# Four edits in a two-layer encoder trunk: kept keys and values, unscaled first products, two heads' states on a diagonal, a stacked rank-16 gate

## The chip, the cores and the metric

The kernel is one launch on one core of a Trainium2 chip. The metric is device microseconds per execution, lower is better. A profiled execution gives a trace of the engines: TensorE's multiplications (PE) and its weight loads (PEld), VectorE (DVE), ScalarE (ACT), GpSimd (POOL) and the queue of SyncE that issues the transfers (SP).

## The reference, cut to what matters

Two layers on x of 1024 positions by 1024 channels, all in float32. Each layer normalises x, multiplies it by one wide matrix and splits the columns among three branches: a gated MLP (u, v, z), an attention with low-rank queries, keys and values (8 heads, causal by chunks of 64), and a gated linear attention (GLA, 4 heads with keys of 64 and values of 128). The branches are gated, added and projected.

```python
h = _rmsnorm(x, norm_g[l])              # x * rsqrt(mean(x*x)) * gain, by position
(u_a, v_a, z_a, c_q, c_kv, k_r, z_b, q_c, k_c, v_c, g_c, z_c, gate_logits) = _split_cols(h @ w_in[l])
# attention: q of a position sees all k, v of its chunk and of earlier ones
# GLA, per head: log_a = log_sigmoid(g_c @ w_gate + b) / 16     (g_c has 16 columns)
#   o = (causal part inside the chunk) + q_t @ state
#   state = decay * state + k_s^T @ v
```

## The kernel before, in words

Positions lie in two halves `h` of 512 columns. A product in float32 is made of three products in the one-pass format fp32r: each operand is split into a high part (ScalarE copy) and a low part (subtraction on VectorE), and high x high, low x high and high x low are added in PSUM (`pair` at L497, `split` at L479). A product on plain float32 operands shows as two PE records.

`build` (L1523) lists segments for each layer; `weave` (L514) strews side work between the main products. `Recorder` (L55) only notes the operations. `Order` (L123) then writes one fixed order for every engine's queue: it gives each operation a due time worked back from the products that need it, and a cost, a latency and the free buffers of a shared pool `g` of 94 tiles (L1624). The trace therefore shows all instructions at L1612, and tiles by the names `g`, `mm`, `sc`, `tr`, `av` (the last four are PSUM).

The places that the change and the prediction touch:

- `side_h` (L698) normalises one half: loads of 8 tiles of x, squares on ScalarE and their sums on VectorE, a column sum on TensorE (`stat`), the power -1/2 on GpSimd, a broadcast by a product (`bcast`), then for each tile a multiplication by gain and scale and a split (`mult`). In layer 0 all of half 0 stands ahead of the first product.
- `natural` (L632) is the product with positions as rows: 8 tiles of x, 4 blocks of positions, 3 products each. It makes `main_n1` (L755, 432 columns: low-rank queries, keys and the rank-16 gate input) and `main_va` (L1211, 512 columns), for half 0, then `main_n1` and `main_va` for half 1.
- `side_c` (L795) transposes the 16 gate columns (`gT`), and `side_gates` (L822) multiplies them by the 16 x 256 gate matrix (`wgu`, loaded in `params`, L422), in plain float32 with 16 rows of contraction: 2 products of 512 columns in each of 4 calls.
- `side_core` (L1030) is GLA for a pair of heads `p` and a half: 8 calls over both layers. `state` (L1069) runs the state over the 4 blocks of 128 positions, the two heads in rows 0 to 63 and 64 to 127 of one tile. `o(e)` (L1088), for each head, makes 4 blocks of 128 columns, each from the product inside the chunk (`at` x `vc`, 128 rows of contraction) and that of q with the state (64 rows).
- `side_att` (L1309) is the attention of one half. For each head of half 1, `loads` (L1315) reads the queries, and the keys of both halves; `head_T` (L1342) transposes, scales and splits them; `vsplit` (L1386) splits the values of both halves. The keys and values of half 0 have been through the same steps when half 0 was done.

```python
self.mm(ps[:, c], st["at"][e][:, b], st["vc"][b][:, e * 128:(e + 1) * 128], True, False)
self.mm(ps[:, c], qa[hd, b].rearrange("p c s -> p (c s)"), st["S"][b][hd], False, True)
```

Of the kernel before, what the change touches and what calls it, by code (L numbers as in the profile page):

```python
# [10 lines left out]
F32 = mybir.dt.float32  # L11
# [9 lines left out]
S = 1024  # L21
# [287 lines left out]
class Builder:  # L309
# [29 lines left out]
    def setup(self):  # L339
        nc, cp, I = self.nc, self.cp, self.I  # L340
        self.ident = cp.tile([128, 128], F32, name="ident")
        make_identity(nc, self.ident)
        self.ones = cp.tile([128, 128], F32, name="ones")
        nc.vector.memset(self.ones, 1.0)
        self.mhalf = cp.tile([128, 8], F32, name="mhalf")
        nc.vector.memset(self.mhalf, -0.5)
        self.half = []
        for e in range(2):
            t = cp.tile([128, 128], F32R, name=f"half{e}")
            nc.vector.memset(t.bitcast(F32), 0.0)  # L350
            nc.vector.memset(t[:, 64 * e:64 * e + 64].bitcast(F32), 1.0)
            self.half.append(t)
        self.zero = cp.tile([128, 128], F32, name="zero")
        nc.vector.memset(self.zero, 0.0)

# [66 lines left out]
    def params(self, l):  # L422
        nc, I = self.nc, self.I
        P = self.P[l]

        def ld(name, src, shape):
            t = self.par.tile(list(shape), F32, tag="p_" + name, name=f"{name}{l}", bufs=2)
            self.load(t, src)
            P[name] = t
            return t  # L430

        ld("bg", I["bg"][l], (128, 24))
        ld("cqg", I["cqg"][l], (128, 2))
        ld("ckvg", I["ckvg"][l], (128, 1))
        ld("wgu", I["wgu"][l], (16, 256))
        ld("lng", I["lng"][l], (128, 4))
        ld("bgu", I["bgu"][l], (128, 2))
        ld("og", I["og"][l], (128, 1))
        nb = self.par.tile([128, 2], F32, tag="p_nbgu", name=f"nbgu{l}", bufs=2)
        nc.vector.tensor_scalar(out=nb, in0=P["bgu"], scalar1=-1.0, scalar2=None, op0=ALU.mult)  # L440
        P["nbgu"] = nb
        for n in ("bg", "og"):
            nc.vector.tensor_scalar(out=P[n], in0=P[n], scalar1=0.5, scalar2=None, op0=ALU.mult)
        for x in ("q", "k"):
            gr = ld(x + "gr", I[x + "gr"][l:l + 1].broadcast_to((128, 32)), (128, 32))
# [186 lines left out]
    def natural(self, u, key, width, evac, order=(0, 1)):  # L632
# [3 lines left out]
        def part(h, k):  # L636
            def f():
# [4 lines left out]
                wh, wl = w[k]  # L642
                hh, hl = u["h"][h][k]
                for t in range(NB):
# [7 lines left out]
                if k == 7:  # L652
                    evac(h, box["p"])
            return f

# [41 lines left out]

    def side_h(self, u, h):  # L698
        nc, l = self.nc, u["l"]
# [20 lines left out]
        def stat():  # L720
            ps = self.ps("tr")
            for t in range(NB):
                self.mm(ps[:, t:t + 1], st["s"][:, t * 128:(t + 1) * 128], self.ones[:, 0:1])
            v = self.s((128, NB), "hv")
            nc.vector.tensor_scalar(out=v, in0=ps[:, 0:NB], scalar1=1.0 / D, scalar2=EPS, op0=ALU.mult, op1=ALU.add)
            r = self.s((128, NB), "hr")
            self.rsqrt(r, v)
            dg = st["d"] = self.g()
# [23 lines left out]

        return [loads, sq(range(0, 4)), sq(range(4, 8)), stat, bcast] + [mult(k) for k in range(8)]

    def main_n1(self, u):  # L755
        def evac(h, pss):
# [3 lines left out]
            for t in range(NB):  # L760
                nat = self.g((128, 432))
                self.evac(nat, pss[t])
                s["nat"].append(nat)
# [31 lines left out]
    def side_c(self, u, h):  # L795
        nc, l = self.nc, u["l"]
        s = u["s"][h]
        def gT():
            ps = self.ps("tr")
            for t in range(NB):  # L800
                self.tr(ps[0:16, t * 128:(t + 1) * 128], s["nat"][t][:, 416:432])
            s["gT"] = self.g((16, H))
            nc.vector.tensor_copy(out=s["gT"], in_=ps[0:16])

# [101 lines left out]
    def side_ukv(self, u, h, t):  # L906
# [40 lines left out]
        return fn  # L947

    def evac(self, out, ps):
        self.nc.scalar.copy(out=out, in_=ps)  # L950
# [79 lines left out]
    def side_core(self, u, p, h):  # L1030
# [38 lines left out]
        def state():  # L1069
            dd = u["kt", p, h][3]  # L1070
            U = self.ps("tr")
            for b in range(nu):
                for e in range(2):
                    hd = slice(e * 64, e * 64 + 64)
                    self.mm(U[hd, b * 128:(b + 1) * 128], st["ksn"][:, b * 128 + e * 64:b * 128 + e * 64 + 64],
                            st["vc"][b][:, e * 128:(e + 1) * 128])
            sts = [self.carry[l, p] if h else self.zero]
            big = self.g((128, NB, 128))
            for b in range(nu):
                nx = big[:, b]  # L1080
                if b == NB - 1:
                    nx = self.carry[l, p] = self.s((128, 128), "S", bufs=2)
                nc.vector.scalar_tensor_tensor(out=nx, in0=sts[-1], scalar=dd[:, b:b + 1],
                                               in1=U[:, b * 128:(b + 1) * 128], op0=ALU.mult, op1=ALU.add)
                sts.append(nx)
            st["S"] = sts

        def o(e):  # L1088
            def f():
                qa = u["qt", p, h][0]  # L1090
                hd = slice(e * 64, e * 64 + 64)
                ps = self.ps("sc")
                for b in range(NB):
                    c = slice(b * 128, b * 128 + 128)
                    self.mm(ps[:, c], st["at"][e][:, b], st["vc"][b][:, e * 128:(e + 1) * 128],
                            True, False)
                    self.mm(ps[:, c], qa[hd, b].rearrange("p c s -> p (c s)"), st["S"][b][hd], False, True)
                jk = self.g()
# [8 lines left out]
                                        in1=r.unsqueeze(2).broadcast_to((128, NB, 128)), op=ALU.mult)  # L1107
                st["on"][e] = on
            return f

        def fin(e):
            def f():
                ps = self.ps("tr")
                for b in range(NB):
                    self.tr(ps[:, b * 128:(b + 1) * 128], st["on"][e][:, b])
                y = u.pop(("zc", h, 2 * p + e))
# [94 lines left out]
    def main_va(self, u):  # L1211
        def evac(h, pss):
            for t in range(NB):
                v = self.g()
                self.evac(v, pss[t])
                d = u["vad", h, t] = self.spill("va")
# [92 lines left out]
    def side_att(self, u, h):  # L1309
# [5 lines left out]
        def loads(hd):  # L1315
            x = X[hd] = {}
            cs = slice(hd * 96, (hd + 1) * 96)
            x["n"] = []
            for src in [self.qd[l, h]] + [self.kd[l, f] for f in range(nf)]:
                t4 = self.g((128, NB, 96))  # L1320
                self.load(t4, src[:, :, cs].rearrange("t p d -> p t d"))
                x["n"].append(t4)
            if hd % 2 == 0:
                z = X["z", hd // 2] = self.g()
                self.load(z, u["zbd", h, hd // 2])
                x["v"] = []
                for f in range(nf):
                    vn = self.g((128, NB, 128))
                    self.load(vn, self.vd[l, f][:, :, hd * 64:hd * 64 + 128].rearrange("t p d -> p t d"))
                    x["v"].append(vn)  # L1330
            else:
                x["v"] = X[hd - 1]["v"]

        def masks(hd):
            x = X[hd]
            x["hi"] = []
            for i in range(nf + 1):
                hi = self.g((KM, H), F32R)
                self.load(hi[RM:KM].bitcast(F32), self.cmask[1 + i if i else h])
                x["hi"].append(hi)  # L1340

        def head_T(hd, i):  # L1342
            x = X[hd]
            nat = x["n"][i]
            gain = self.P[l]["gvk" if i else "gvq"]
            ps = self.ps("tr")
            for t in range(NB):
# [4 lines left out]
                                           op1=ALU.subtract)  # L1352
            x["T", i] = (hi, lo)

        def mx(hd, b):
# [30 lines left out]
        def vsplit(hd):  # L1386
# [3 lines left out]
            vs, os = slice(64 * e, 64 * e + 64), slice(64 - 64 * e, 128 - 64 * e)  # L1390
            for vn in x["v"]:
                V = self.g((128, NB, 128), F32R)
                self.split(V[:, :, vs], V[:, :, os], vn[:, :, vs])
                x["V"].append(V)

# [56 lines left out]
        def preps(hd):  # L1452
            out = [lambda: masks(hd)] + [lambda i=i: head_T(hd, i) for i in range(nf + 1)]
            out += [lambda b=b: mx(hd, b) for b in range(NB)]
# [22 lines left out]
        side += [lambda a=a: av(*a) for a in steps[-AVLAG:]]  # L1477
        n0 = 1 + 1 + nf + 1 + NB + 3 + 1
        return side[:n0], side[n0:]
# [43 lines left out]
    def build(self):  # L1523
# [22 lines left out]
        for i, u in enumerate(units):  # L1546
# [6 lines left out]
            if i == 0:  # L1553
                sh = self.side_h(u, 0)
# [137 lines left out]
```

## Time and profile before

| | |
|---|---|
| three executions, median (lowest to highest) | 2029.34 us (2029.3 to 2030.12) |
| the profiled execution | 2029.29 us, span of its instructions 2027.6 us |
| PE, DVE, ACT, POOL busy | 99%, 76%, 50%, 27% of the span |
| moved by DMA | 302.13 MB, 149 GB/s in the mean |

In the trace, PE x16 means 16 records in a row. Ends of products are modelled, so a busy PE may still be slower than its pace. The chain of waits follows the work that ended last back from its end; a row of it tells which engine set the pace in that stretch, and for how long.

### The profile page before, as it was taken

To read this page: it belongs to the slowest core of one execution; us is meant where nothing else is said; L and a number is where in the kernel's file an instruction comes from. 1 tells how busy PE (TensorE), PEld (TensorE's weight loads), DVE (VectorE), ACT (ScalarE), POOL (GpSimd) and SP (SyncE) were. 2 spreads that over 40 slices of the span, in tenths; PEclk is the share of its full clock that TensorE was granted. 3 is DMA by queue.
4 is the path that set the end of the run, shared out by engine and by line. 5 is a ranking of instruction groups with operands and counts; after the bars stand their busy time and mean duration, and the time that the engine had idled before them with its cause. 6 is when DMAs were issued, how large, how long until landed. Compare 5 with 4: busy or idle time off the path is not lost.

```text
span 2027.6 us, 29291 instructions
## 1 busy us (share of the span) xinstructions
PE 2000.4 (99%) x9864; PEld 1648.0 (81%) x9864; DVE 1543.7 (76%) x2779; ACT 1011.8 (50%) x1969; POOL 542.2 (27%) x460
## 2 busy tenths in 40 slices
PE   6999999999999999999999999999999999999999
PEld 5887778888888878888889877788888887887887
DVE  7576666867778988997845856578678799889973
ACT  6565344455456644555434653345445565444541
POOL 1110101001123446665012001110011344567630
PEclk9999999999999999999999999999999999999999
DMA  7262234343533755426743613334435338463362
GB/s 242 87 228 79 73 110 161 130 156 133 185 123 105 244 178 185 131 100 199 248 150 105 206 60 103 110 135 163 138 130 194 112 101 288 133 214 117 102 211 89
DMA packets 216326, 302.13 MB, mean 149 GB/s; under 512 B 63176, under 2 KB 91880, under 8 KB 216176
## 3 DMA queue, kind: packets, MB, share of 16 engines
q1 hardware_dynamic: 216176, 300.26, 44.9%
q8 instruction: 78, 1.28, 0.3%
q14 instruction: 72, 0.59, 0.1%
HBM read 207.76 MB, written 92.43 MB: 148 GB/s over the span
## 4 chain that ended last, share of the span: by engine, by line
PE 91%; DVE 6%; POOL 1%; ACT 1%; issue 1%; DMA 0%; SPq 0%; DVEq 0%; POOLq 0%; ACTq 0%
PE mm L1612 68%; PE sc L1612 10%; PE tr L1612 7%; PE av L1612 6%; DVE g L1612 5%; POOL g L1612 1%; DVE mx L1612 1%; ACT g L1612 1%; DMA g<-xT 0%; POOL hr L1612 0%; DVE negm L1612 0%; SPq L1612 0%; DVE hv L1612 0%; DVEq L1612 0%; POOLq L1612 0%
## 5 line engine op out<-in xcount | busy, mean ns | idle before, releaser
L1612 PE MATMUL mm<-g,g 128*128 128x512 f32 (+1 forms) x6480 | 1588.4, 393 | 2.9 <-ACT g L1612 2.2
L1612 PEld LDWEIGHTS mm<-g,g 128*128 128x128 f32 x6480 | 1197.9, 188 | 248.1 <-issue 5.5
L1612 DVE TENSOR_TENSOR g<-g,g 128x512 fp32r<-128x512 f32 (+5 forms) x1053 | 755.8, 750 | 137.4 <-ACT g L1612 122.9
L1612 POOL TENSOR_TENSOR g<-g,g 128x256 f32<-128x256 f32 (+5 forms) x352 | 419.1, 1211 | 364.4 <-ACT g L1612 260.1
L1612 ACT CAST g<-g 128x512 fp32r<-128x512 f32 (+3 forms) x704 | 401.6, 601 | 229.7 <-DVE g L1612 180.0
L1612 ACT ACTIVATE g<-sc 128x512 f32<-128x512 f32 (+5 forms) x432 | 200.8, 510 | 241.3 <-PE sc L1612 231.6
L1612 PE MATMUL sc<-g,g 64*64 64x64 f32 (+8 forms) x1632 | 264.3, 298 | 0.0
L1612 PEld LDWEIGHTS sc<-g,g 64*64 64x64 f32 (+4 forms) x1632 | 202.8, 172 | 37.9 <-issue 4.7
L1612 DVE TENSOR_TENSOR g<-mm,g 128x512 f32<-128x512 f32 (+1 forms) x176 | 117.5, 673 | 124.3 <-PE mm L1612 74.5
L1612 ACT COPY g<-mm 128x512 f32<-128x512 f32 (+1 forms) x168 | 97.0, 580 | 227.3 <-PE mm L1612 218.2
L1612 PE MATMUL av<-g,g 128*128 128x512 f32 (+3 forms) x672 | 183.9, 362 | 0.3 <-POOL g L1612 0.3
L1612 ACT ACTIVATE g<-g 128x512 f32<-128x512 f32 (+3 forms) x225 | 129.2, 589 | 81.3 <-DVE g L1612 64.2
L1612 PEld LDWEIGHTS av<-g,g 128*128 128x128 f32 x672 | 122.4, 189 | 19.0 <-POOL g L1612 2.1
L1612 DVE SCALAR_TENSOR_TENSOR g<-g,g 128x512 f32<-128x512 f32 (+3 forms) x185 | 129.9, 711 | 7.7 <-ACT g L1612 6.5
L1612 DVE TENSOR_REDUCE mx<-tr 128x1 f32<-128x512 f32 (+1 forms) x192 | 105.0, 570 | 14.9 <-PE tr L1612 13.1
L1612 DVE SCALAR_TENSOR_TENSOR g<-g,mm 128x512 f32<-128x512 f32 x112 | 76.1, 681 | 46.9 <-PE mm L1612 31.0
L1612 PE MATMUL tr<-g,g 128*64 128x128 f32 (+5 forms) x416 | 100.8, 342 | 3.5 <-DVE mx L1612 2.1
L1612 POOL TENSOR_TENSOR qr<-qv,mhalf 128x8 f32<-128x8 f32 x16 | 29.0, 1812 | 280.0 <-DVE qv L1612 280.0
L1612 PEld LDWEIGHTS tr<-g,g 115*128 115x128 f32 (+2 forms) x416 | 62.0, 174 | 25.6 <-DVE mx L1612 6.9
L1612 POOL TENSOR_SCALAR_AFFINE_SELECT g<-g 128x512 f32<-128x512 f32 x16 | 12.3, 768 | 248.8 <-ACT g L1612 243.7
L1612 PE MATMUL tr<-ident,g 128*96 128x128 f32 (+2 forms) x480 | 76.4, 272 | 0.4 <-issue 0.4
L1612 PEld LDWEIGHTS tr<-ident,g 128*96 128x96 f32 (+2 forms) x480 | 57.2, 128 | 17.2 <-issue 1.2
(119 smaller groups left out, 886.6 us busy)
## 6 DMA issues: line engine op xcount, KB each, us to landing
g<-wT SPq DMA_DIRECT2D x176, 256.0 KB
sg<-g SPq DMA_DIRECT2D x96, 256.0 KB
g<-sg SPq DMA_DIRECT2D x96, 256.0 KB
g<-wbr SPq DMA_DIRECT2D x64, 256.0 KB
g<-wo SPq DMA_DIRECT2D x64, 256.0 KB
g<-kd SPq DMA_DIRECT2D x48, 192.0 KB
g<-xT SPq DMA_DIRECT2D x32, 256.0 KB
hd<-g SPq DMA_DIRECT2D x32, 256.0 KB
```

The lines of the kernel that those rows point to most:

```text
L1612: ins = real[op.i] = fn(*a, **k)
```

## The change

Four edits. **Kept keys and values:** half 0's attention stores the transposed, split keys and the split values of each head (three transfers), and half 1's loads them instead of making them again. **Unscaled first products:** in layer 0, the products of half 0 in `main_n1` and `main_va` take x times gain, split without the scale by position; the scale is applied by ScalarE where PSUM is read (`evac_n`). The scaled tiles are still made, later. **Diagonal:** the states of two heads lie on the diagonal of a 128 x 256 tile with zeros beside them, so one product with 128 rows and 256 columns serves both heads; where the state is zero it is left out. **Gate:** high, low and high part of the gate input lie at rows 0, 32 and 64 of one 80-row tile, the high, high and low part of the matrix beside them, so one fp32r product with 80 rows replaces the float32 product.

```diff
# params
-        ld("wgu", I["wgu"][l], (16, 256))
+        w = self.g((80, 256))
+        self.nc.gpsimd.memset(w, 0.0)
+        for r in (0, 32, 64):
+            self.load(w[r:r + 16], I["wgu"][l])
...
+        self.nc.scalar.copy(out=P["wgu"], in_=w)
+        self.nc.vector.tensor_tensor(out=P["wgu"][64:80], in0=w[64:80], in1=P["wgu"][64:80].bitcast(F32),
+                                     op=ALU.subtract)
# natural
-                hh, hl = u["h"][h][k]
+                hh, hl = (u.get(("raw", h)) or u["h"][h])[k]
# side_h
+        def rough(k):
+            def f():
+                gain = self.P[l]["ng"][:, k:k + 1]
+                x, hi, lo = st["x"][k], self.g(dt=F32R), self.g(dt=F32R)
+                nc.scalar.activation(out=hi, in_=x, func=AF.Copy, scale=gain)
+                nc.vector.scalar_tensor_tensor(out=lo, in0=x, scalar=gain, in1=hi.bitcast(F32), op0=ALU.mult,
+                                               op1=ALU.subtract)
+                u.setdefault(("raw", h), []).append((hi, lo))
+            return f
...
+        if early:
+            out[1:1] = [rough(k) for k in range(8)]
# side_c
-            s["gT"] = self.g((16, H))
-            nc.vector.tensor_copy(out=s["gT"], in_=ps[0:16])
+            g = s["gT"] = self.g((80, H), F32R)
+            nc.gpsimd.memset(g.bitcast(F32), 0.0)
+            nc.scalar.copy(out=g[0:16], in_=ps[0:16])
+            nc.scalar.copy(out=g[64:80], in_=ps[0:16])
+            nc.vector.tensor_tensor(out=g[32:48], in0=ps[0:16], in1=g[0:16].bitcast(F32), op=ALU.subtract)
# new, called where main_n1 and main_va read PSUM
+    def evac_n(self, u, h, t, out, ps):
+        if ("raw", h) in u:
+            self.nc.scalar.activation(out=out, in_=ps, func=AF.Copy, scale=u["r", h][:, t:t + 1])
+        else:
+            self.evac(out, ps)
# side_core: state
-                nc.vector.scalar_tensor_tensor(out=nx, in0=sts[-1], scalar=dd[:, b:b + 1],
-                                               in1=U[:, b * 128:(b + 1) * 128], op0=ALU.mult, op1=ALU.add)
+            big = [self.g((128, 2, 256)) for _ in range(2)]
+            own = lambda b, e: big[b // 2][e * 64:e * 64 + 64, b % 2, e * 128:(e + 1) * 128]
+            for t in big:
+                nc.gpsimd.memset(t[0:64, :, 128:256], 0.0)
+                nc.gpsimd.memset(t[64:128, :, 0:128], 0.0)
...
+                for e in range(2):
...
+                        nc.vector.scalar_tensor_tensor(out=nx, in0=own(b, e), scalar=dd[hd, b:b + 1], in1=uc,
+                                                       op0=ALU.mult, op1=ALU.add)
# side_core: o, now by pairs of blocks i instead of by head e
+                for b in (2 * i, 2 * i + 1):
+                    c = (b % 2) * 256
+                    past = h or b
+                    if past:
+                        self.mm(ps[:, c:c + 256], qa[:, b].rearrange("p c s -> p (c s)"), st["S"][b], True, False, True)
+                    for e in range(2):
+                        self.mm(ps[:, c + e * 128:c + (e + 1) * 128], st["at"][e][:, b],
+                                st["vc"][b][:, e * 128:(e + 1) * 128], not past, True, True)
# side_att: masks, head_T, vsplit (loads drops half 0's keys and values)
+            if h:
+                lo = self.g((96, H), F32R)
+                kh, kl, _ = u["kept", hd]
+                self.load(x["hi"][1][0:96].bitcast(F32), kh[0:96])
+                self.load(lo.bitcast(F32), kl[0:96])
+                x["T", 1] = (x["hi"][1], lo)
...
+            if i and not h:
+                u["kept", hd] = [self.spill("kept") for _ in range(3)]
+                for d, t in zip(u["kept", hd], (hi[0:96], lo)):
+                    self.store(d[0:96], t.bitcast(F32))
...
+            if h:
+                V0 = self.g((128, NB, 128), F32R)
+                self.load(flat(V0), u.pop(("kept", hd))[2])
+                x["V"].append(V0)
+            else:
+                self.store(u["kept", hd][2], flat(V))
# build, layer 0
-                segs.append(([], [sh[0], lambda: self.par_ng(0), sh1[0]] + sh[1:], 0, 1))
-                sh1 = sh1[1:5] + [lambda: self.params(0)] + sh1[5:] + [self.setup2]
+                segs.append(([], [sh[0], lambda: self.par_ng(0), sh1[0]] + sh[1:9], 0, 1))
+                sh1 = sh[9:] + sh1[1:5] + [lambda: self.params(0)] + sh1[5:] + [self.setup2]
-            segs.append((n1[:8] + va[:8], sh1, 0.0, 0.7))
+            segs.append((n1[:8] + va[:8], sh1, 0.0 if i else 0.15, 0.7))
```

## Rows read from the trace of the kernel before

**Rows 1.** The page, part 1: busy time, share of the span and instructions.

```profile
PE 2000.4 (99%) x9864; PEld 1648.0 (81%) x9864; DVE 1543.7 (76%) x2779; ACT 1011.8 (50%) x1969; POOL 542.2 (27%) x460
```

**Rows 2.** Waits of PE: who for whom, us in total, times, longest.

```profile
PE tr L1612 <- DVE g L1612: 16.4, 5, 12.4
PE mm L1612 <- ACT g L1612: 2.2, 1, 2.2
PE tr L1612 <- DVE mx L1612: 2.1, 4, 0.6
```

**Rows 3.** The chain of waits, 0 to 60 us: start us, us, what.

```profile
1.71 5.32 DMA g<-xT
...
12.45 1.88 PE tr L1612 x8
...
20.63 1.45 PE mm L1612 x3
22.08 0.36 PE av L1612
22.44 2.07 PE mm L1612 x6
...
27.06 0.11 PE tr L1612 x2
...
27.47 0.56 PE tr L1612 x6
...
31.86 0.86 PE tr L1612 x2
...
43.08 2.08 PE mm L1612 x9
45.16 0.68 PE av L1612 x3
```

**Rows 4.** The chain of waits, 200 to 260 us, in the GLA stretch.

```profile
206.06 3.14 PE sc L1612 x16
...
211.46 0.22 PE sc L1612 x2
...
211.92 0.41 PE sc L1612 x2
...
222.33 2.75 PE mm L1612 x12
...
243.39 2.95 PE mm L1612 x12
```

**Rows 5.** The chain of waits, 402 to 409 us: float32 products with 128 rows.

```profile
402.56 0.89 PE sc L1612 x8
```

**Rows 6.** The chain of waits, 120 to 130 us, around two gate products.

```profile
124.34 1.91 PE sc L1612 x4
126.25 2.27 PE mm L1612 x9
...
129.20 2.04 PE mm L1612 x9
```

**Rows 7.** The chain of waits, 751 us: one head's four transposes.

```profile
751.64 0.44 PE tr L1612 x4
```

**Rows 8.** DVE's groups by form, 0 to 65 us: busy us, mean ns.

```profile
L1612 DVE TENSOR_TENSOR g<-g,g 128x512 fp32r<-128x512 f32 x25 | 16.5, 686 | 1.8 <-ACT g L1612 1.8
L1612 DVE SCALAR_TENSOR_TENSOR g<-g,ng,g 128x512 f32<-128x512 f32 x16 | 11.4, 747 | 0.6 <-ACT g L1612 0.6
L1612 DVE TENSOR_TENSOR g<-g,g 128x432 fp32r<-128x432 f32 x8 | 4.7, 603 | 0.0
```

**Rows 9.** Windows: stretch; PE, PEld, DVE, ACT, POOL busy; clock; DMA.

```profile
200.00:325.00 125.00, 125.00 (x776) 97.95 (x775) 76.26 (x139) 46.83 (x83) 15.66 (x16) 1.00 0.28 91
740.00:940.00 200.00, 198.63 (x949) 162.97 (x947) 175.54 (x237) 101.80 (x209) 136.71 (x107) 1.00 0.44 140
```

**Rows 10.** The state tile: one update on DVE (ns min/median/max).

```profile
L1612 DVE SCALAR_TENSOR_TENSOR g<-S,dd,tr x4: 348/348/349, 232.6 to 1309.2; 128x128 f32<-128x128 f32 x4
```

**Rows 11.** The chain of waits, 840 to 885 us, in half 1's attention.

```profile
844.93 3.93 DVE g L1612 x5
...
871.03 5.15 DVE g L1612 x6
```

**Rows 12.** DVE's groups by form, 740 to 940 us: keys, and halves of values.

```profile
L1612 DVE TENSOR_TENSOR g<-g,g 128x256 fp32r<-128x256 f32 x14 | 10.4, 771 | 0.0
L1612 DVE SCALAR_TENSOR_TENSOR g<-tr,gvk,g 96x512 fp32r<-96x512 f32 x12 | 8.5, 724 | 1.1 <-ACT g L1612 1.0
```

**Rows 13.** Waits of the SP queue, 740 to 940 us.

```profile
SPq L1612 <- DVE g L1612: 57.3, 18, 9.7
```

More of the change, by code (lines that the diff above doesn't have):

```diff
@@ L352, in setup @@
             self.half.append(t)
-        self.zero = cp.tile([128, 128], F32, name="zero")
-        nc.vector.memset(self.zero, 0.0)
     def setup2(self):
@@ L434, in params @@
         ld("ckvg", I["ckvg"][l], (128, 1))
-        ld("wgu", I["wgu"][l], (16, 256))
+        w = self.g((80, 256))
+        self.nc.gpsimd.memset(w, 0.0)
+        for r in (0, 32, 64):
+            self.load(w[r:r + 16], I["wgu"][l])
+        P["wgu"] = self.par.tile([80, 256], F32R, tag="p_wgu", name=f"wgu{l}", bufs=2)
+        self.nc.scalar.copy(out=P["wgu"], in_=w)
+        self.nc.vector.tensor_tensor(out=P["wgu"][64:80], in0=w[64:80], in1=P["wgu"][64:80].bitcast(F32),
+                                     op=ALU.subtract)
         ld("lng", I["lng"][l], (128, 4))
@@ L653, in f @@
                     evac(h, box["p"])
+                    if key == "wva":
+                        u.pop(("raw", h), None)
             return f
@@ L696, in side_t, with side_h @@
         return out
-    def side_h(self, u, h):
+    def side_h(self, u, h, early=False):
         nc, l = self.nc, u["l"]
@@ L723, in stat @@
                 self.mm(ps[:, t:t + 1], st["s"][:, t * 128:(t + 1) * 128], self.ones[:, 0:1])
-            v = self.s((128, NB), "hv")
+            v = self.s((128, NB), "hv", bufs=4)
             nc.vector.tensor_scalar(out=v, in0=ps[:, 0:NB], scalar1=1.0 / D, scalar2=EPS, op0=ALU.mult, op1=ALU.add)
-            r = self.s((128, NB), "hr")
+            r = self.s((128, NB), "hr", bufs=4)
             self.rsqrt(r, v)
+            u["r", h] = r
             dg = st["d"] = self.g()
@@ L751, in mult @@
             return f
-        return [loads, sq(range(0, 4)), sq(range(4, 8)), stat, bcast] + [mult(k) for k in range(8)]
+        def rough(k):
[7 more added lines that the diff above has]
+            return f
+        out = [loads, sq(range(0, 4)), sq(range(4, 8)), stat, bcast] + [mult(k) for k in range(8)]
+        if early:
+            out[1:1] = [rough(k) for k in range(8)]
+        return out
     def main_n1(self, u):
@@ L761, in evac @@
                 nat = self.g((128, 432))
-                self.evac(nat, pss[t])
+                self.evac_n(u, h, t, nat, pss[t])
                 s["nat"].append(nat)
@@ L1076, in state @@
                             st["vc"][b][:, e * 128:(e + 1) * 128])
-            sts = [self.carry[l, p] if h else self.zero]
-            big = self.g((128, NB, 128))
-            for b in range(nu):
-                nx = big[:, b]
-                if b == NB - 1:
-                    nx = self.carry[l, p] = self.s((128, 128), "S", bufs=2)
-                nc.vector.scalar_tensor_tensor(out=nx, in0=sts[-1], scalar=dd[:, b:b + 1],
-                                               in1=U[:, b * 128:(b + 1) * 128], op0=ALU.mult, op1=ALU.add)
-                sts.append(nx)
@@ L1086, in state @@
-            st["S"] = sts
-        def o(e):
+            big = [self.g((128, 2, 256)) for _ in range(2)]
[3 more added lines that the diff above has]
+                nc.gpsimd.memset(t[64:128, :, 0:128], 0.0)
+            carry = None
+            if h:
+                for e in range(2):
+                    nc.scalar.copy(out=own(0, e), in_=self.carry[l, p][e * 64:e * 64 + 64])
+            else:
+                carry = self.carry[l, p] = self.s((128, 128), "S", bufs=2)
@@ new lines, in state @@
+            for b in range(nu):
+                for e in range(2):
+                    hd = slice(e * 64, e * 64 + 64)
+                    nx = carry[hd] if b == NB - 1 else own(b + 1, e)
+                    uc = U[hd, b * 128:(b + 1) * 128]
+                    if b == 0 and not h:
+                        nc.vector.tensor_copy(out=nx, in_=uc)
+                    else:
+                        nc.vector.scalar_tensor_tensor(out=nx, in0=own(b, e), scalar=dd[hd, b:b + 1], in1=uc,
+                                                       op0=ALU.mult, op1=ALU.add)
@@ L1089, in f, with o @@
+            st["S"] = [big[b // 2][:, b % 2] for b in range(NB)]
+        def o(i):
             def f():
                 qa = u["qt", p, h][0]
-                hd = slice(e * 64, e * 64 + 64)
                 ps = self.ps("sc")
[L1093 to L1097, printed above, removed]
+                for b in (2 * i, 2 * i + 1):
[3 more added lines that the diff above has]
+                        self.mm(ps[:, c:c + 256], qa[:, b].rearrange("p c s -> p (c s)"), st["S"][b], True, False, True)
+                    for e in range(2):
+                        self.mm(ps[:, c + e * 128:c + (e + 1) * 128], st["at"][e][:, b],
+                                st["vc"][b][:, e * 128:(e + 1) * 128], not past, True, True)
@@ L1107, in f @@
                                         in1=r.unsqueeze(2).broadcast_to((128, NB, 128)), op=ALU.mult)
-                st["on"][e] = on
+                st["on"][i] = on
             return f
@@ L1114, in f @@
                 for b in range(NB):
-                    self.tr(ps[:, b * 128:(b + 1) * 128], st["on"][e][:, b])
+                    self.tr(ps[:, b * 128:(b + 1) * 128], st["on"][b // 2][:, b % 2 * 2 + e])
                 y = u.pop(("zc", h, 2 * p + e))
@@ L1214, in evac @@
                 v = self.g()
-                self.evac(v, pss[t])
+                self.evac_n(u, h, t, v, pss[t])
                 d = u["vad", h, t] = self.spill("va")
@@ L1318, in loads @@
             x["n"] = []
-            for src in [self.qd[l, h]] + [self.kd[l, f] for f in range(nf)]:
+            for src in (self.qd[l, h], self.kd[l, h]):
                 t4 = self.g((128, NB, 96))
@@ L1325, in loads @@
                 self.load(z, u["zbd", h, hd // 2])
[L1326 to L1330, printed above, removed]
+                vn = x["v"] = self.g((128, NB, 128))
+                self.load(vn, self.vd[l, h][:, :, hd * 64:hd * 64 + 128].rearrange("t p d -> p t d"))
             else:
@@ L1340, in masks @@
                 x["hi"].append(hi)
+            if h:
[4 more added lines that the diff above has]
+                x["T", 1] = (x["hi"][1], lo)
         def head_T(hd, i):
             x = X[hd]
-            nat = x["n"][i]
+            nat = x["n"][min(i, 1)]
             gain = self.P[l]["gvk" if i else "gvq"]
@@ L1390, in vsplit @@
             vs, os = slice(64 * e, 64 * e + 64), slice(64 - 64 * e, 128 - 64 * e)
[L1391 to L1394, printed above, removed]
+            flat = lambda t: t.rearrange("p a b -> p (a b)").bitcast(F32)
+            vn = x["v"]
+            V = self.g((128, NB, 128), F32R)
+            self.split(V[:, :, vs], V[:, :, os], vn[:, :, vs])
+            if h:
+                V0 = self.g((128, NB, 128), F32R)
+                self.load(flat(V0), u.pop(("kept", hd))[2])
+                x["V"].append(V0)
+            else:
+                self.store(u["kept", hd][2], flat(V))
+            x["V"].append(V)
         def qk(hd, kb):
@@ L1452, in preps @@
         def preps(hd):
-            out = [lambda: masks(hd)] + [lambda i=i: head_T(hd, i) for i in range(nf + 1)]
+            out = [lambda: masks(hd)] + [lambda i=i: head_T(hd, i) for i in (0, nf)]
             out += [lambda b=b: mx(hd, b) for b in range(NB)]
@@ L1477, in side_att @@
         side += [lambda a=a: av(*a) for a in steps[-AVLAG:]]
-        n0 = 1 + 1 + nf + 1 + NB + 3 + 1
+        n0 = 1 + 1 + 2 + NB + 3 + 1
         return side[:n0], side[n0:]
@@ L1553, in build @@
             if i == 0:
-                sh = self.side_h(u, 0)
-                segs.append(([], [sh[0], lambda: self.par_ng(0), sh1[0]] + sh[1:], 0, 1))
-                sh1 = sh1[1:5] + [lambda: self.params(0)] + sh1[5:] + [self.setup2]
+                sh = self.side_h(u, 0, True)
+                segs.append(([], [sh[0], lambda: self.par_ng(0), sh1[0]] + sh[1:9], 0, 1))
+                sh1 = sh[9:] + sh1[1:5] + [lambda: self.params(0)] + sh1[5:] + [self.setup2]
             g0, c0 = self.side_c(u, 0)
```

## The prediction

> **What bounds the kernel now.** The page's table of busy times comes first: PE is busy for 2000.4 us of 2027.6 [rows 1]. The waits of PE come next. They name 16.4 us for a VectorE tile, 12.4 of it in one piece, and 2.2 us for ScalarE; what else they name is small [rows 2]. The chain of waits shows where those lie: the first product of the first stage starts at 20.63 us, behind loads, sums and a normalisation [rows 3]. Behind that point PE runs to the end almost without a gap. So an edit is worth what it takes out of PE's stream, plus what it takes off the start. Work of the other engines counts only where it is late. A busy PE is not a PE at its pace, though, so I read each price from the chain, where a run of records has a start and a length.
>
> **The diagonal.** One block of `o` is 16 records, 8 of q with the state (64 rows of contraction) and 8 inside the chunk (128 rows), and takes 3.14 us [rows 4], so 0.196 us a record. Alone, two 128-row records take 0.22 us and two 64-row records 0.41 [rows 4], and eight 128-row records of the same width elsewhere take 0.89, that is 0.111 each [rows 5]. So the 64-row records are the dear ones, and dearest between 128-row ones: (3.14 - 8 x 0.111) / 8 = 0.28 us each. The twelve products behind a block take 2.95 us instead of 2.75 [rows 4]: 0.2 us more for each of 16 blocks, 3.2 us.
>
> After the change every record has 128 rows. No row shows a float32 product of 128 rows and 256 columns. A float32 record of 512 columns takes 1.91 / 4 = 0.478 us [rows 6], half of that is 0.239; twice a record of 128 columns is 0.222. I take 0.239, since half of a wide record holds no more small costs than it should. A block then has 4 such records and 8 of 0.111: 0.956 + 0.89 = 1.85 us. In four blocks the first state is zero and two records fall away, 4 x 2 x 0.239 = 1.9 us. The sum: 16 x (3.14 - 1.85) + 1.9 + 3.2 = **25.7 us**. The upper end, with 0.222, is 26.8. The lower end is a chunk record that stays at 0.196 whatever stands beside it: a block of 2.52 us, and 16 x 0.62 + 1.9 = 11.8 us.
>
> On VectorE each state update becomes two of half the rows. An update takes 0.348 us [rows 10], and I take the same for half the rows, since the columns are the same: 28 more, 9.7 us, in two stretches like that from 200 to 325 us, where DVE is busy for 76.26 of 125 us [rows 9]. GpSimd's four memsets a call lie in the same stretch, where it is busy for 15.66. Both are hidden; without that cover the state chain would be late by some 1.4 us a call.
>
> The Trainium skill ("TensorE: Matmul & The Clock Gate", the table of Why this matters for your kernels) says that a lone product with K=32 takes as long as one with K=128, and that the gain of small K lies in tiles that run side by side. It speaks against this edit: by it the padded form saves nothing beside the 1.9 us, and the sum would be some 24 us shorter.
>
> **The gate.** Two float32 products of 16 rows and 512 columns take 1.91 us [rows 6]. One fp32r product of 512 columns takes 2.75 / 12 = 0.229 [rows 4]. Eight of them save 8 x (0.955 - 0.229) = 5.8 us. The nine products behind take 2.27 us instead of 2.04 [rows 6], and four such places add 0.9: **6.7 us**, between 5.8 and 6.7. The extra copies, memsets, loads and the subtraction lie on queues that nobody waits for there; uncovered, they are under a microsecond for each half.
>
> **Kept keys and values.** Each of 16 heads of half 1 loses four transposes of 0.44 us [rows 7]: **7.0 us** of PE. VectorE loses a key split of 0.72 us and a value split of 0.77 at most [rows 12], ScalarE their copies. In that stretch DVE is busy for 175.54 of 200 us [rows 9], and the chain runs over it in pieces of 3.9 and 5.2 us [rows 11], so PE waits there in its modelled busy time. 16 x 1.49 = 24 us leave VectorE; the most that PE can get back I put at a third, 8 us, the least at nothing, and I take **2 us**, since the order on the queues is fixed anew and one relieved wait uncovers the next. The SP queue gets three stores and three loads per head and loses one and a half loads. They are issued a head ahead; where the cover is gone, the first score of a head waits (a rival).
>
> **The start.** The first tile of x has landed well before the third, which was issued at 1.71 us and landed 5.32 later [rows 3]; the first weight tile will be about the third load. With its split, a first product is possible at 7.03 + 0.55, near 7.5 us, where 0.55 is a little under the split's 0.603 on DVE [rows 8]; at the best it starts at 5. Before, the first half's 96 products and half 1's two statistics ran from 20.63 to 43.08: 22.45 us [rows 3], slow first products among them (3.88 us for ten, where the pace later is half of that), which I leave in. Half 0's statistics lay ahead of that and now stand in the stream: by half 1's rows 0.11 + 0.56 + 0.86 = 1.5 us [rows 3]. So the second stage starts at 7.5 + 22.45 + 1.5 = 31.5 instead of 43.08: 11.6 us earlier. For gaps between the first tiles I take 0.6 off: **11 us**, at the best 14.
>
> What can hold it back is VectorE. Until half 1's first product it must make 8 raw low parts (6.0 us at 0.747), 8 splits of narrow weights (4.8), 8 of wide ones (5.5), 14 sums and 2 diagonals (11), and the scaled tiles of half 0 and one of half 1 (9 x 1.43 = 13) [rows 8]: 40 us. It has from 5 us to 31.5 + 8 x (2.08 + 0.68) = 53.6 us [rows 3], 48 us, less the small work of the tables. If the new 6 us are all late, the start brings 5.
>
> **The sum.** 25.7 + 6.7 + 7.0 + 2 + 11 = 52.4 us. The profiled execution took 2029.29 us (its span 2027.6, so 1.7 around it), 0.05 under the median of the three runs. 2029.29 - 52.4 = 1976.9, rounded to **1977 us**.
>
> **Rivals.** (a) *The start is held by VectorE:* it brings 5 instead of 11, 1983 us. For it speaks 40 of 48 us of work, against it that weights and raw tiles are due first in the planner's order. (b) *Attention goes at VectorE's pace:* PE's 7.0 + 2 us there come back as waits, 1986 us. For it, [rows 9, 11]; against it, that VectorE loses more than PE does. (c) *The 64-row form is not the cause:* the blocks of `o` keep their length because of the order of their records, only 1.9 us come, 1977 + 23.8 = 2001 us. This is the time by the skill's rule of equal cost; against it speak the pairs of 0.22 and 0.41 us, which stand apart from each other [rows 4]. (d) *Slower:* the kept tiles come late. Every transfer is on the one SP queue, which stops at a store whose data is not ready; from 740 to 940 us it waited 57.3 us for VectorE, 9.7 in one piece [rows 13]. If a reload stands behind such a store, the head's first score waits, and PE behind it. It decides from 52.4 / 16 = 3.3 us a head; 9.7 us at every second head is 78 us, 2055 us. Against it: no product now waits for a transfer by name [rows 2]. (e) *The fixed order shifts so that new waits eat everything:* 2029 us.
>
> **Chances.** What this kernel's measurement can tell from no change is about 0.2%, 4 us. The forecast (all terms near their values, 1964 to 1988): 0.62. (a) 0.12, (b) 0.12, (c) 0.07, all faster: 0.93. (e) 0.03 no change. (d) 0.04 slower. The range starts at 1964 (start 14, attention 8, diagonal 26.8, gate and transposes as taken: 62.5 off is 1966.8, and a little beyond) and reaches to 1996, past (a) and (b) together (1992) and the bound of the diagonal's lower end alone (1977 + 13.9 = 1991); (c), (d) and (e) stay out, 0.14, and some 0.04 below.
>
> **What would show it.** In the profile after: PE's first product near 7.5 us; blocks of `o` with 12 records in about 1.85 us, and no 2.95 behind them; gate products of about 0.23 us and 2.04 behind them; 256 key and query transposes instead of 320; PE still busy nearly all the time behind the start. The prediction is wrong if a block stays near 3 us, if PE's waits name transfers in the attention, or if a wait of several microseconds stands ahead of half 1's first product.

## The result, and the profile after

The changed kernel takes 1982.14 us in the median of 4 executions (1978.91 to 1984.6), the kernel before 2029.49: a ratio of 0.9765, with a 95% interval from 0.9748 to 0.9782. The forecast was 1977, with 1964 to 1996 as the range. The profiled execution took 1982.53 us, 46.8 under the one before.

The page of the changed kernel, part 1, against [rows 1]:

```profile
PE 1959.3 (99%) x9720; PEld 1630.7 (82%) x9720; DVE 1540.4 (78%) x2784; ACT 1007.6 (51%) x1963; POOL 555.8 (28%) x498
```

PE lost 144 records: 8 of the gate, 72 of the states and 64 transposes, and it is as full as it was.

The chain of waits of the changed kernel, first 0 to 60 us, then the GLA stretch, in the columns of [rows 3]:

```profile
8.40 6.25 ACT g L1670 x11
14.65 0.01 issue
14.66 0.74 DVE g L1670 x2
...
16.66 0.83 PE tr L1670 x6
...
22.25 3.83 ACT g L1670 x7
26.08 0.73 DVE g L1670 x2
...
29.68 1.22 DVE g L1670 x2
...
33.15 3.75 PE mm L1670 x9
36.90 0.69 PE av L1670 x3
...
38.29 0.86 PE tr L1670 x2
...
41.23 2.04 PE mm L1670 x9
...
286.85 2.96 PE mm L1670 x12
289.81 1.75 PE sc L1670 x12
291.56 2.77 PE mm L1670 x12
294.33 1.75 PE sc L1670 x12
```

The second stage starts at 33.15 us instead of 43.08 [rows 3], but from the first product on the chain ahead of it runs over ScalarE and VectorE too, no longer over PE alone, and its first nine products take 3.75 us instead of 2.08. A block of `o` is 12 records in 1.75 us instead of 16 in 3.14, and the twelve products behind it take 2.77 us instead of 2.95 [rows 4]. (The 2.96 us of the first line at 286.85 stand behind a run of transposes, not behind a block of `o`.)

The waits of PE, against [rows 2], and windows of the first stage, in the columns of [rows 9]:

```profile
PE mm L1670 <- ACT g L1670: 5.9, 3, 5.2
PE mm L1670 <- DVE g L1670: 3.3, 3, 1.1
PE tr L1670 <- DVE g L1670: 2.8, 3, 1.6
...
PE sc L1670 <- DVE g L1670: 1.7, 2, 0.8
```

```profile
10.00:15.00 5.00, 4.64 (x23) 3.79 (x21) 5.00 (x9) 5.00 (x10) 0.00 (x0) 1.00 1.04 380
15.00:20.00 5.00, 3.38 (x21) 3.26 (x21) 4.09 (x9) 3.63 (x8) 1.54 (x2) 1.00 1.05 382
20.00:25.00 5.00, 5.00 (x25) 4.35 (x25) 3.75 (x7) 2.75 (x6) 0.04 (x1) 1.00 1.01 365
25.00:30.00 5.00, 4.51 (x22) 3.67 (x20) 5.00 (x9) 4.23 (x8) 0.00 (x0) 1.00 0.59 178
30.00:35.00 5.00, 4.06 (x19) 3.63 (x20) 4.81 (x9) 3.49 (x7) 1.44 (x1) 0.82 0.39 122
35.00:40.00 5.00, 5.00 (x18) 3.66 (x18) 4.95 (x9) 5.00 (x19) 0.01 (x1) 0.84 0.33 121
```

The one long wait is now the 5.2 us ahead of the first product. No transfer stands in the list. New are 1.7 us ahead of gate products. The granted clock, 1.00 in both windows of [rows 9], is 0.82 and 0.84 in the last two of these: it stood at the lower of its two levels (1.2 of 2.4 GHz) for part of them, behind pauses of PE of 0.28 and 1.15 us that ended at 30.94 us, and (0.18 + 0.16) x 5 = 1.7 us went that way.

Where the time went can be read from starts alone, without the modelled ends. The same 512-column products of tile `mm` run in the same stages in both kernels. I took the start of the n-th of them from the trace of PE, record by record, and subtracted it from its start before: what is gained up to that product, in us. `rows128` is an experiment below, `part_*` are the kernel before with one edit each.

```
n-th product (before at)   changed  rows128  part_diag  part_gate  part_kept  part_start
  20  (48.6, stage 2)          7.3      8.6        1.0       0.0        0.2         7.4
 200  (140.1, one gate pair)   7.9      9.2        1.0       0.5        0.3         7.4
 400  (195.1, two pairs)       9.7     11.0        1.0       2.3        0.3         7.4
 800  (332.3, GLA done)       23.0     24.0       14.3       2.3        0.3         7.4
3050  (1012.5, layer 1 done)  27.5     28.4       14.3       2.2        5.3         7.2
3150  (1060.8, layer 2 begun) 26.2     28.4       14.3       2.2        4.1         6.0
4000  (1361.1, GLA done)      41.9     43.8       27.6       4.6        4.1         6.0
6180  (2020.8)                46.9     48.6       27.6       5.2        9.1         5.8
```

The GLA stretches and the attention bring what they should: 13.3 us in each layer for the diagonal, and 4.5 to 5.1 for the attention. (The changed kernel's 15.7 us from the 3150th product to the 4000th hold layer 2's gate as well.) The start brings less, and 1.3 us are lost again at the beginning of layer 2, where the clock fell once more (last section).

### The profile page after: what moved, and what is told of

It is laid out like the page before. It is cut to its first block, busy times and chain, and to the rows that moved or that the text cites. A ratio compares the mean times of both kernels' runs of the same rounds, so it can differ in the third digit from the quotient of the medians.

```text
span 1980.8 us, 29262 instructions
## 1 busy us (share of the span) xinstructions
PE 1959.3 (99%) x9720; PEld 1630.7 (82%) x9720; DVE 1540.4 (78%) x2784; ACT 1007.6 (51%) x1963; POOL 555.8 (28%) x498
## 4 chain that ended last, share of the span: by engine, by line
PE 87%; DVE 6%; POOL 3%; issue 2%; ACT 1%; DMA 0%; SPq 0%; POOLq 0%; DVEq 0%; ACTq 0%
PE mm L1670 67%; PE sc L1670 8%; PE tr L1670 6%; PE av L1670 5%; DVE g L1670 4%; POOL g L1670 2%; ACT g L1670 1%; DVE mx L1670 1%; POOL qr L1670 0%; POOL krr L1670 0%; DVE negm L1670 0%; DMA g<-xT 0%; DVE qv L1670 0%; DVE kv L1670 0%; DMA g<-wo 0%
## 5 line engine op out<-in xcount | busy, mean ns | idle before, releaser
L1670 DVE TENSOR_TENSOR g<-g,g 128x512 fp32r<-128x512 f32 (+4 forms) x1037 | 745.3, 750 | 118.4 <-ACT g L1670 107.7
L1670 ACT CAST g<-g 128x512 fp32r<-128x512 f32 (+2 forms) x688 | 396.2, 606 | 218.2 <-DVE g L1670 159.7
L1670 PE MATMUL sc<-g,g 64*64 64x64 f32 (+8 forms) x1592 | 248.1, 297 | 0.0
L1670 PEld LDWEIGHTS sc<-g,g 128*128 128x128 f32 (+3 forms) x1592 | 197.6, 172 | 29.6 <-issue 4.3
L1670 DVE SCALAR_TENSOR_TENSOR g<-g,g 128x512 f32<-128x512 f32 (+3 forms) x185 | 122.7, 675 | 6.9 <-ACT g L1670 5.4
L1670 PE MATMUL tr<-ident,g 128*96 128x128 f32 (+2 forms) x416 | 69.3, 273 | 0.0
L1670 PEld LDWEIGHTS tr<-ident,g 128*96 128x96 f32 (+2 forms) x416 | 50.1, 128 | 16.8 <-DVE g L1670 1.0
L1670 ACT ACTIVATE g<-g,bg 128x512 f32<-128x512 f32 x72 | 52.0, 722 | 23.2 <-DVE g L1670 23.1
```

Of the source, the lines that this page charges most:

```text
L1670: ins = real[op.i] = fn(*a, **k)
```

## The experiments

**One edit at a time.** Each kernel is the one before with only those parts of the diff that belong to one edit: diagonal (`setup`, `state`, `o`, `fin`), gate (`params`, `gT`), kept tiles (`side_att`), start (the rest).

```diff
 part_diag:   + big = [self.g((128, 2, 256)) ...]      o(i) by pairs of blocks
 part_gate:   + P["wgu"] of 80 rows, g = s["gT"] = self.g((80, H), F32R)
 part_kept:   + u["kept", hd] stored in half 0, loaded in half 1
 part_start:  + rough(k), evac_n, side_h(u, 0, True)
```

> The kernel before with the diagonal states alone. Theory (the edits work apart, each at the price its records have): a block of the GLA output falls from 3.14 us to about 1.8, the twelve products behind it from 2.95 to 2.75; the time falls by 26 us (25 to 27), to about 2003.5 us. Rival (the gain in the GLA stretch of the changed kernel leans on the other edits, or VectorE's doubled state updates stall it): blocks shorter, but less than 22 us off the whole.

> The kernel before with the stacked gate alone. Theory: eight products go from 0.955 to 0.24 us and the 0.23 us behind each of four pairs go too: 6 to 7 us off, about 2023 us. Rival: its longer preparation (memset, two copies, a subtraction) is late for the first product of each layer, and 2 to 4 us of it come back: 2025 to 2027 us.

> The kernel before with the kept keys and values alone. Theory: 64 transposes of 0.11 us (7.0 us) and some of the waits for VectorE in the attention: 9 to 11 us off, about 2019.5 us. Rival 1: only the transposes: 7 us off, 2022.5 us. Rival 2 (the reloads come late on the SP queue): under 5 us off, with waits of PE for a transfer by name.

> The kernel before with the unscaled first products alone. Theory: the first product at about 5 us instead of 20.6, 10 us gained at the first product of the second stage, and 2 to 4 us lost again while VectorE catches up: 6 to 8 us off, about 2022.5 us; executions with a full granted clock throughout lie about 2 us under those with a dip near 35 us. Rival: the loss of the changed kernel came from the other edits' new order, and this one alone keeps its 10 to 11 us: about 2018.5 us.

Measured, against 2029.63 us for the kernel before on the same chip:

| edit alone | us | less by | ratio, 95% interval | term of the prediction |
|---|---|---|---|---|
| diagonal | 2003.1 | 26.5 | 0.9869 (0.9855 to 0.9884) | 25.7 |
| gate | 2024.97 | 4.7 | 0.9977 (0.9968 to 0.9987) | 6.7 |
| kept tiles | 2020.88 | 8.8 | 0.9957 (0.9942 to 0.9972) | 7.0 + 2 |
| start | 2023.46 | 6.2 | 0.9971 (0.9959 to 0.9984) | 11 |

The four add up to 46.2 us, the whole change to 47.4: they work apart. The diagonal and the kept tiles are at their terms; the interval of the kept tiles, 5.7 to 11.8 us, holds the rival of 7 us as well, so that its 2 us rest on the positions above. The gate lies at the edge of its rival, with 2 us back, and the start at its theory, well under the term of the prediction. But the start's way there was another than its theory had: 8.4 us, not 10, at the first product of the second stage, then 1.0 lost by the 20th and 1.2 at the beginning of layer 2, where the granted clock fell; between those two places hardly anything was lost (0.2 us). In `part_kept` no wait of PE names a transfer, so reloads on the SP queue don't hold it up.

In `part_gate` the wait stands where the rival had it. Its waits of PE and its chain, 100 to 130 us:

```profile
PE sc L1622 <- DVE g L1622: 0.9, 1, 0.9
```

```profile
116.60 1.99 POOL qr L1622
...
120.84 1.65 POOL krr L1622
...
124.23 0.84 DVE g L1622 x2
125.10 0.69 DVE g L1622
125.93 0.47 PE sc L1622
126.40 1.61 PE mm L1622 x7
```

Before, this stretch of the chain was PE alone up to the gate product at 124.34 [rows 6]. Now it runs through the normalisation of the last queries and keys (powers on GpSimd, then VectorE), and the last VectorE piece, 0.69 us, is the new subtraction, which VectorE reaches behind them. The subtraction takes no longer than what it replaced. The kernel before had a copy in its place, on VectorE too; the timelines of before and of `part_gate`:

```profile
123.35 0.67 DVE L1612 COPY g<-tr 16x512 f32<-16x512 f32 x1
...
125.10 0.68 DVE L1622 TENSOR_TENSOR g<-tr,g 16x512 fp32r<-16x512 f32 x1
```

The copy ended more than a microsecond ahead of the product that needs it (half 1's, the second of the pair). ScalarE's two copies of the gate input, the first of which the subtraction needs, had ended at 122.98 us in `part_gate`, so it could have stood where the copy stood; the order of VectorE's queue put it 1.75 us later, behind more query and key work and a subtraction of 128 rows. It is its place in the order that PE waits for, not its length.

**Is it the 64 rows?** The wide product of the changed kernel is cut in two again, so a block has 16 records as before the change, but all of them with 128 rows.

```diff
-                    if past:
-                        self.mm(ps[:, c:c + 256], qa[:, b].rearrange("p c s -> p (c s)"), st["S"][b], True, False, True)
                     for e in range(2):
+                        if past:
+                            self.mm(ps[:, c + e * 128:c + (e + 1) * 128], qa[:, b].rearrange("p c s -> p (c s)"),
+                                    st["S"][b][:, e * 128:(e + 1) * 128], True, False, True)
```

> The changed kernel, with each 256-column product of q and the diagonal state cut into two of 128 columns, both with 128 rows (half of them zeros): 16 records a block again, as before the change. Theory (the 64-row form is the cause): every record takes 0.11 us, a block 16 x 0.111 = 1.78 us, the time stays within 2 us of the changed kernel, about 1981 us. Rival (the number or the alternation of the records is the cause): a block near 3.1 us, some 20 us slower, about 2002 us.

Measured: 1980.78 us, a ratio of 0.9759 (0.9743 to 0.9775). The chain of `rows128`, 284 to 300 us:

```profile
285.79 2.96 PE mm L1671 x12
288.75 1.78 PE sc L1671 x16
290.54 2.74 PE mm L1671 x12
```

Sixteen records in 1.78 us, 0.111 each, where the same number with half of them at 64 rows took 3.14. So neither the number nor the alternation of the records was the cause: it was the 64-row form between 128-row ones, and the 256-column product as such gives next to nothing more (0.03 us a block).

**What holds the start.** Two shifts of the changed kernel's side work, and the changed kernel once more beside them.

```diff
 late_mult:
-                sh1 = sh[9:] + sh1[1:5] + [lambda: self.params(0)] + sh1[5:] + [self.setup2]
+                sh1 = sh[9:13] + sh1[1:5] + [lambda: self.params(0)] + sh1[5:] + sh[13:] + [self.setup2]
 sums_late:
-            segs.append((n1[:8] + va[:8], sh1, 0.0 if i else 0.15, 0.7))
+            segs.append((n1[:8] + va[:8], sh1, 0.0 if i else 0.3, 0.7))
```

> The changed kernel, with half 0's scaled tiles (8 multiplications and 8 splits, 11.4 us of VectorE) noted behind half 1's instead of ahead of them in the first stage. Theory (VectorE holds the start): its waits between 12 and 40 us go, the second stage starts 1 to 3 us earlier, and the dip of the granted clock near 35 us goes or gets rarer: 1976 to 1980 us. Rival 1 (ScalarE and the loads hold it): no change, 1981 to 1983 us. Rival 2: half 1's first products, or the stage that reads half 0's tiles, then wait: slower than 1984 us.

> The changed kernel, with the side work of the first stage begun at 0.3 of it instead of 0.15, so that half 0's sums of squares are due later than the raw tiles. Theory (PE's order puts the column sum ahead of products that are ready): the 1.6 us that PE waits near 15 us goes, and the second stage starts 1 to 2 us earlier: 1979 to 1980.5 us. Rival: the scale then comes late for the reading of PSUM, the wait moves to the end of the first products, and nothing is won: 1981 to 1983 us.

> The changed kernel itself once more, beside the other two on the same chip: 1979 to 1985 us; every execution with a granted clock of 1.000 near 1979, those at 0.998 and 0.997 some 3 and 5 us above, since each dip holds the half clock for about 3.4 us and costs about 1.7 us.

Measured: `late_mult` 1981.84 us (0.9766, 0.9751 to 0.978), `sums_late` 1982.99 (0.9771, 0.9758 to 0.9785), the changed kernel 1980.51 (0.9764, 0.9749 to 0.9779). No gain in either: the first is where its rival 1 had it, the second where its rival had it. But the windows show two different reasons. `late_mult`, then `sums_late` with its waits of PE:

```profile
15.00:20.00 5.00, 3.88 (x19) 3.33 (x18) 3.93 (x8) 3.73 (x8) 1.66 (x2) 0.79 1.06 379
20.00:25.00 5.00, 3.88 (x15) 2.87 (x14) 3.50 (x7) 2.47 (x5) 0.00 (x0) 0.87 0.72 220
...
30.00:35.00 5.00, 5.00 (x25) 4.35 (x24) 4.33 (x12) 2.17 (x5) 0.00 (x0) 1.00 0.21 64
```

```profile
25.00:30.00 5.00, 1.12 (x2) 0.29 (x2) 4.79 (x8) 3.28 (x7) 0.00 (x0) 1.00 0.22 69
30.00:35.00 5.00, 4.49 (x20) 4.25 (x20) 4.55 (x8) 3.52 (x8) 0.00 (x0) 0.66 0.34 106
```

```profile
PE mm L1670 <- ACT g L1670: 9.9, 2, 5.6
```

In `late_mult` PE is full from 30 us on, where the changed kernel has 4.06 of 5: VectorE's early tiles did cause that wait. But PE still pauses between 15 and 20 us, and between 20 and 25, where the changed kernel is full, it has a new wait of 1.1 us for ScalarE; the clock dipped there. Its pauses behind the first product add up to 2.6 us; in the two profiles of the changed kernel they are 3.4 (above) and 2.5 (`after_again`). In `sums_late` the pause near 15 us is gone and comes back between 25 and 30 us with 3.9 us (4.4 in all, up to 30.5), as its rival said. The trace names ScalarE for it (9.9 us in two waits, the first of them the 5.6 us ahead of the first product): it is ScalarE that reads PSUM with the scale. The pause was moved, not removed.

**The gate's wait**, alone and with the other shifts:

```diff
-            segs.append((n1[8:] + va[8:], [self.side_w(u), g0] + c0 + uq(0), 0.0, 1.0))
-            segs.append((vc, [g1, self.side_gates(u, 0)] + self.side_t(u), 0.0, 0.95))
+            segs.append((n1[8:] + va[8:], [self.side_w(u), g0] + c0 + uq(0)[:5] + [g1] + uq(0)[5:], 0.0, 1.0))
+            segs.append((vc, [self.side_gates(u, 0)] + self.side_t(u), 0.0, 0.95))
```

> The changed kernel, with the gate input of half 1 prepared earlier: its transposes, copies and subtraction are noted in the middle of the stage before, not at its end. Theory (the first gate product of each layer waits because the new subtraction stands on VectorE's queue behind the last key and value work): PE's wait of 0.8 us ahead of the 80-row product goes, with what hides in front of it, and 1 to 2.5 us come over two layers: 1978 to 1980 us. Rival (the wait is that last key and value work itself, whatever the gate does): no change, 1980.5 to 1982 us.

> The changed kernel with half 0's scaled tiles noted behind half 1's, and the gate input earlier. Theory: the gate's 1 to 2.5 us, and nothing or half a microsecond from the start: 1978 to 1980.5 us. Rival: as the changed kernel, 1980.5 to 1982 us.

> All three shifts together. Theory: 2 to 4 us under the changed kernel, 1977 to 1979 us, with no wait of PE of more than 1 us between the first product and 100 us. Rival: the waits only move, 1980 to 1982 us.

Measured, against 2028.73 us: `gate_early` 1979.03 (0.9761, 0.9748 to 0.9774), `gate_and_mult` 1980.14 (0.9759, 0.9746 to 0.9772), `all_three` 1981.15 (0.9762, 0.9749 to 0.9776). The first two lie in the ranges of their theories and the third in its rival's, but all overlap with the changed kernel's 0.9764 (0.9749 to 0.9779), so none of them is shown to beat it. In `all_three` a wait of 1.7 us for ScalarE stands behind the first product, where its theory had none of more than 1 us.

In `gate_early` the named wait is gone, and in its place a product into a PSUM tile `tr` waits 0.55 us, for the same subtraction, which again stands behind query and key work in VectorE's order. Its chain, then its timeline:

```profile
95.67 1.65 POOL qr L1670
97.34 1.02 DVE g L1670 x2
```

```profile
99.52 0.68 DVE L1670 TENSOR_TENSOR g<-tr,g 16x512 fp32r<-16x512 f32 x1
...
100.25 0.96 PE L1670 MATMUL tr<-g,g 128*128 128x512 f32 x3 [0.55 <-DVE g L1670]
```

By positions its gain falls from 9.5 to 7.5 us between the 50th and the 100th product and is 10.3 at the 200th; since no wait but this one stands there, most of the fall is work that was moved ahead and is missing behind. The changed kernel on the same scale (the run `after_again`) goes 8.0, 8.0, 8.5. From the 50th to the 200th product the earlier gate input is worth 0.80 - 0.55 = 0.25 us, in layer 2 (3150th to 3300th product) 0.87 - 0.53 = 0.34. So this move has a small part of the gate's missing 2 us. Giving the subtraction the place in VectorE's order that the copy had was not tried.

## Why the prediction was right

**The bound, right.** PE set the end before and after, at 99% of the span; each edit was worth what it took from PE's stream, and less where PE then had to wait. None of the three signs of being wrong came: the blocks are at 1.75 us, no wait of PE names a transfer, and half 1's first product lies in a stretch, from 30.94 us to the gate's wait at 118 us, in which PE has no wait.

**The diagonal, right in mechanism and size.** 25.7 us forecast, 26.5 measured alone. By positions it is 26.6 in the two GLA stretches; 1.0 us more lies ahead of the second stage, where this edit only drops one memset and two profiles of the changed kernel differ by as much, so I don't count it. The block takes 1.75 us, not 1.85, as the 256-column record costs (1.75 - 8 x 0.111) / 4 = 0.216 us: near the bound from twice a 128-column record (0.222), not the half of a 512-column one (0.239) that I took. The 0.2 us behind each block went too. Rival (c) fell twice: in the trace, and in `rows128`. The Trainium skill's rule that a single product with K=32 takes as long as one with K=128 ("TensorE: Matmul & The Clock Gate", Why this matters for your kernels) does not carry over to these 64-row records: by it I had estimated 2001 us, measured 1982. VectorE's doubled state updates take 0.347 us each and stayed hidden: no wait of PE in that stretch.

**The kept tiles, right, the 2 us partly by luck.** 7.0 + 2 forecast, 8.8 alone, 9.1 by the position of the products. PE's transposes with 96 columns went from 320 records to 256. By positions each layer's attention brings 5.0 us in `part_kept`, of which 32 transposes are 3.5. Of the other 1.5, about 1.2 lie in the 115-row products into tile `tr`, of which VectorE takes the maxima: from start to start they got shorter, while PE's waits by name hardly changed (2.7 and 2.5 us). That fits VectorE's relief, but no run takes the relief alone. So 3 us came where I took 2, and a dip of the clock at the beginning of layer 2 took 1.2 back. Rivals (b) and (d) didn't come about: the gain stayed, and no wait of PE names a transfer.

**The gate, mis-sized by 2 us.** A product takes 0.47 / 2 = 0.24 us, as forecast. The step that failed is that the preparation's queues are ones "that nobody waits for there". The first pair of each layer comes right behind VectorE's last query and key work. The subtraction stands 1.75 us later in VectorE's order than the copy that it replaced, PE waits 0.85 us for it, and about 1 us of what that pair should bring (2 x (0.955 - 0.24) + 0.23 = 1.66) was lost in each layer: `part_gate` gains 0.5 at its first pair and 1.8 at its second.

**The start, mis-sized: 11 forecast, 6.2 alone.** The first product came sooner than I took, at 5.22 us instead of 7.5, and the second stage still began later, at 33.15 instead of 31.5. The step that failed is the 0.6 us for gaps, and the count by which VectorE has 48 us for 40 us of work. The total fits, but the order doesn't: VectorE was busy for the whole of 10 to 15 us and of 25 to 30 us, in the order of the planner's due times, and PE stopped for it or for ScalarE four times: 0.36, 1.62, 0.28 and 1.15 us, 3.4 together, the two long ones for VectorE. And I had put both statistics of half 1 ahead of 43.08 us; after the change the second of them, the broadcast, 0.86 us, lies behind the start of the second stage, so that the 9.9 us gained there are worth 9. From the first product to the second stage 27.9 us passed: 22.45 + 1.5 - 0.86 + 3.4 = 26.5, and 1.4 that the products took beyond my 22.45, for which the runs give no reason. A dip of the clock took 1.7 more behind the start of the second stage, which leaves the 7.3 us of the table, and a second dip at the beginning of layer 2 leaves 6.0. Rival (a) named the engine of the two long pauses. Its price, 5 us, is near what was measured by luck: it stood for 6 us of late raw tiles, and what came were pauses, two dips and a broadcast, against a first product 2.3 us sooner.

**The sum.** 26.5 + 4.7 + 8.8 + 6.2 = 46.2 from single edits against 52.4 forecast; the whole change gave 47.4.

## What to carry to other kernels

Read the price of a small product from where it stands, in a run of its neighbours, and not from its mean duration: here padding with zeros to full rows was worth more than half of the whole change. When an edit lets the bounding engine start earlier, lay the feeding engines' work against it stretch by stretch; that their total fits says little, and a pause that is taken out at one place tends to come back at the next.

## What the runs showed of the hardware that I had not expected

The granted clock can fall to its lower level behind short pauses of PE, and the same pause doesn't always bring it down. At the beginning of layer 2 PE waits 0.99 us for a VectorE tile in the kernel before, in `part_kept` and in both profiles of the changed kernel. Two windows of each, in this order:

```profile
1040.00:1045.00 5.00, 4.19 (x21) 3.41 (x19) 2.05 (x3) 4.38 (x9) 0.00 (x0) 1.00 0.00 0
1045.00:1050.00 5.00, 4.77 (x22) 3.52 (x23) 2.89 (x7) 1.41 (x4) 1.40 (x1) 1.00 0.00 2
...
1035.00:1040.00 5.00, 4.01 (x20) 3.29 (x19) 2.08 (x3) 4.66 (x10) 0.00 (x0) 1.00 0.01 2
1040.00:1045.00 5.00, 5.00 (x19) 4.11 (x20) 3.13 (x6) 0.96 (x2) 1.40 (x1) 0.66 0.01 3
...
1015.00:1020.00 5.00, 4.01 (x22) 3.15 (x21) 2.85 (x5) 3.73 (x8) 1.03 (x1) 0.97 0.00 0
1020.00:1025.00 5.00, 5.00 (x15) 3.48 (x14) 3.26 (x6) 1.39 (x6) 0.38 (x1) 0.69 0.00 0
...
1015.00:1020.00 5.00, 4.01 (x22) 3.19 (x21) 2.68 (x6) 3.04 (x7) 1.40 (x1) 1.00 0.00 0
1020.00:1025.00 5.00, 4.96 (x20) 3.42 (x19) 4.93 (x9) 3.37 (x12) 0.00 (x0) 1.00 0.24 85
```

It fell in `part_kept` and in the first profile of the changed kernel, and stayed at 1.00 in the kernel before and in `after_again`, which is the changed kernel again. All four executions of `part_kept` had a mean clock of 0.999 and all six of `part_start` 0.997 to 0.999, against 1.000 in all four of `part_diag`. For the changed kernel the time follows the clock: 1978.91 us at 1.000, 1981.76 and 1982.53 at 0.998, 1984.6 at 0.997. Why one pause is followed by a dip and the same one in another execution is not, these runs don't settle. The kernel before had 1.000 in 29 of the 31 executions beside the experiments, and 0.999 in two. Without the dips the changed kernel is at 1979 to 1980 us.
